# Adding the sent expert rows to the shared expert's rows by accumulating transfers of GpSimd's queue

## The chip, the cores and the metric

The kernel runs on one core of one Trainium2 chip. The metric is the device time of one execution in microseconds (us), the median of several runs. Its engines are TensorE (PE in the profile; PEld is its weight load), VectorE (DVE), ScalarE (ACT), GpSimd (POOL) and SyncE (SP), which does nothing here but issue transfers. GpSimd and ScalarE issue transfers as well. SPq in the rows is SyncE's queue.

## What is computed

One decoder layer for 512 tokens of width 1024, all in float32: a mixer (attention and short convolution), and then a mixture of experts with a shared expert. Only the second half matters here:

```python
h = h + rms_norm(mix, post_mix_norm)
t = rms_norm(h, pre_ffn_norm)                       # 512 tokens x 1024
# each token: the best of 4 groups, and in it the 2 best of 8 experts, weights combine[n, e]
hid = silu(t @ w_gate[e]) * (t @ w_up[e]) * combine[:, e]        # 32 experts, 256 wide
routed = sum over the chosen e of hid @ w_down[e]
shared = (silu(t @ w_sh_gate) * (t @ w_sh_up)) @ w_sh_down
out = h + rms_norm(routed + shared, post_ffn_norm)
```

So each token has two routed rows of 1024 numbers, one from each of its two experts, and one shared row.

## The kernel before

**Experts by pairs.** The 32 experts are worked off in 16 pairs by `pairs_gen`. A pair gathers up to 64 tokens of each of its two experts into 128 partitions (tile `xg`, by an indirect transfer from `t_d` in HBM), multiplies them with the two experts' weights (PSUM tile `pgu`, then `pht`, then `pdn`), and gets 128 finished rows (tile `yb`). For the first 15 pairs `send` puts these rows into `y_d` in HBM with an indirect transfer of GpSimd's queue. `y_d` has 1024 rows: row k\*512 + n holds what token n got from its k-th expert, k = 0 or 1. Rows that have no place there, those of the last pair among them, stay zero.

**Weights.** SyncE's queue loads each expert's three weight tiles of 1024 KB (`ld (e, i)`; i = 2 is the down projection) in the order in which `queue_load` puts them down, into a pool of 25 slots. The last two weights are `ld (31, 2)` and `ld (15, 2)`. Behind them come `gp` (the norm's gain), four loads `kk0` to `kk3` of 1024 KB each, and two loads `hb0` and `hb1` of 1024 KB, which hold the residual h. `kk{c}` brings both `y_d` rows of the 128 tokens of block c side by side. A `kk` load may only be put into the queue once the last send has been issued (`ok=lambda: "sent" in cv`).

**The end.** `shared_gen` has left the shared expert's rows in SBUF, two tiles `sho`, of which `acc(c)` is the part of token block c (c = 0 to 3). The last pair's rows don't go through `y_d`: `last_gen` keeps them in `ys`, split into a high and a low part, and a one-hot matrix `sel` spreads them over the tokens by a product. For each block c and each half of the columns one PSUM bank `pca` adds up three things: the shared rows (`inject`, product of the identity with `acc(c)`), the last pair's rows (product of `sel` with `ys`) and the sent rows (VectorE adds the two halves of `kk{c}`, and a product of the identity with that sum closes the bank). Then ScalarE squares the bank for the norm, VectorE multiplies it with the gain into `tm`, GpSimd raises the mean square to the power -0.5 (`rf`), VectorE adds the residual (`store`, into `hb`), and SyncE writes the block out in two halves.

**Order.** Each engine works off its instructions in the order in which the generators issue them; `run` picks the next generator by estimated times while the program is built. GpSimd's queue is such an order too: a transfer that waits there holds up what stands behind it. At run time an instruction starts when what it waits for has come.

Nearly all instructions are issued through one helper at line 159 (line 314 for products), so tiles, not lines, tell them apart.

Of the kernel before, what the change touches and what calls it, by code (L numbers as in the profile page):

```python
# [13 lines left out]
OP = mybir.AluOpType  # L14
# [4 lines left out]
P = 128  # L19
# [146 lines left out]
def hymba_kernel(ctx: ExitStack, tc: tile.TileContext, xT, xmT, x, meta, cpk, pos, wqkv, wconv, wuq, wukv,  # L166
# [123 lines left out]
    def free_bank(n=1):  # L290
        def f():
            if len(banks) + n <= NBANK:
                return 0.0
            return sorted(done(b) for b in banks)[len(banks) + n - NBANK - 1]
        return f
# [7 lines left out]
    def flag(d, *names):  # L303
        return lambda: 0.0 if all(n in d for n in names) else INF
# [4 lines left out]
    def every(*needs):  # L309
        return lambda: max(f() for f in needs)  # L310
# [64 lines left out]
    def queue_load(name, src, n=2048, ok=None):  # L375

        Slots.queue.append((name, src, n, ok))
# [22 lines left out]
        if j == S_AT:  # L400
            queue_load((NE, 2), we[NE, 2])
    queue_load("gp", g_post[None, :].to_broadcast([P, D]), D)
    for c in range(NT):
        queue_load(f"kk{c}", y_d[:, :].rearrange("(k c p) d -> c p k d", k=2, c=NT)[c], ok=lambda: "sent" in cv)
        if c % 2:
            queue_load(f"hb{c // 2}", h_d[c // 2 * 256:(c // 2 + 1) * 256, :].rearrange("(q p) d -> p q d", p=P))


    jp = m1.bitcast(I32)[:, 0:P]
# [672 lines left out]
    def acc(c):  # L1082
        return sh["out"][c // 2][:, (c % 2) * D:(c % 2 + 1) * D]
# [299 lines left out]
    def overflow():  # L1383

        n = nc.values_load(ov["novf"][0:1, 0:1], min_val=0, max_val=16)  # L1385
        with tc.If(n > 0):
            for half in range(2):
                for c in range(NT):
                    combine(rt["ys"], sel, HALF[half], c)
            for c in range(NT):  # L1390
                V.tensor_tensor(acc(c), acc(c), fin["kk"][c][:, :D], op=OP.add)
            with tc.For_i(0, n, 1) as i:
                overflow_tile(i)
            post_again()
# [62 lines left out]
    def pairs_gen():  # L1457
        wk_, yb, ys, box = rt["wk"], rt["yb"], None, None
        rt["jk"] = wk_.bitcast(BF)[:, 3584:3584 + 512]
        xt_ = wk_[:, :D]  # L1460
        sg, hd, ht = (wk_[:, D + q * 256:D + (q + 1) * 256] for q in range(3))
        yield every(at(xg[0]), free_bank(2))
        xpose(xg[0], xt_)
        gather(2)
        first = NP - PE_PAIRS
        for j, es in enumerate(pairs):
            ps = None
            for i in range(2):
                yield every(loaded(*((e, i) for e in es)), free_bank())
                w = [got((e, i)) for e in es]  # L1470
                yield at(*w, xt_)
                if ps is None:
                    ps = bank("pgu")
                for k in range(4):
                    col2(ps, xt_[:, (4 * i + k) * P:(4 * i + k + 1) * P],
                         [w[q][:, k * 512:(k + 1) * 512] for q in range(2)], i + k == 0, i + k == 4)
                rel(*w)
            hidden(ps, wgt[:, j:j + 1], sg, hd)
            sh["silu"] = True
            if j == S_GO:  # L1480
                sh["go"] = True
            if j == first:
                box = reserve("ys", dt=F32R)
                rel(yb)
                yield lambda: 0.0 if box else INF
                rt["ys"] = ys = box[0]
            if j + 1 < NP:
                yield every(at(xg[(j + 1) % 2]), free_bank(2))
                xpose(xg[(j + 1) % 2], xt_, V)
            if j + 3 < NP:  # L1490
                gather(j + 3)
            if j == NP - 1:
                yield every(flag(sh, "done"), free_bank(2))
                inject(0)
            yield every(at(hd), free_bank())
            hidden_t(hd, ht)
            if j >= first:
                V.tensor_tensor(sel.rearrange("p (c n) -> p c n", c=NT), iop[:, None, :].to_broadcast([P, NT, P]),
                                tok[:, :, j:j + 1].to_broadcast([P, NT, P]), op=OP.is_equal)
            if j == NP - 1:  # L1500
                spawn(last_gen(es), 5)
                return
            yield every(loaded(*((e, 2) for e in es)), free_bank(2))
            w = [got((e, 2)) for e in es]
            yield at(*w, ht)
            for half in range(2):
                ps = down(half, ht, [t[:, half * D:(half + 1) * D] for t in w])
                if j >= first:
                    y_out(ps, ys, HALF[half])
                else:  # L1510
                    o = yb[:, j % 2 * D:(j % 2 + 1) * D][:, HALF[half]]
                    if half:
                        V.tensor_copy(o, ps)
                    else:
                        S.activation(o, ps, AF.Copy)
            rel(*w)
            if j < first:
                send(j, yb[:, j % 2 * D:(j % 2 + 1) * D])
            if j == first - 1:
                cv["sent"] = True  # L1520

    def send(j, y):

# [11 lines left out]
    def inject(c):  # L1535

        for half in range(2):
            pa[c, half] = bank("pca")
            held.append(pa[c, half])
            mm(pa[c, half], ident, acc(c)[:, HALF[half]], start=True, stop=False)  # L1540

    def last_gen(es):


        ys, ht = rt["ys"], rt["wk"][:, D + 512:D + 768]
        ss, rf = small([P, 2 * NT], "ssf"), small([P, NT], "rf")
        var = small([P, 2 * NT], "var")
        kk = {}
        yield every(loaded(*((e, 2) for e in es)), free_bank(2))
        w = [got((e, 2)) for e in es]  # L1550
        yield at(*w, ht)
        for half in range(2):
            y_out(down(half, ht, [t[:, half * D:(half + 1) * D] for t in w]), ys, HALF[half])
        rel(*w)
        yield free_bank(2)
        inject(1)
        tm = reserve("tm0", "tm1")
        yield every(loaded("gp"), lambda: 0.0 if len(tm) == 2 else INF)
        gp, hb = got("gp"), {}
        fin.update(gp=gp, tm=tm, kk=kk)  # L1560

        def rows(c):

            kk[c] = got(f"kk{c}")
            V.tensor_tensor(kk[c][:, :D], kk[c][:, :D], kk[c][:, D:2 * D], op=OP.add)

        def tmc(c, o=slice(0, D)):
            return tm[c // 2][:, c % 2 * D:(c % 2 + 1) * D][:, o]

        def store(c):  # L1570
            if c % 2 == 0:
                hb[c // 2] = got(f"hb{c // 2}")
            h = hb[c // 2][:, c % 2 * D:(c % 2 + 1) * D]
            for q in HALF:
                V.scalar_tensor_tensor(h[:, q], tmc(c, q), rf[:, c:c + 1], h[:, q], op0=OP.mult, op1=OP.add)
                Y.dma_start(out[c * P:(c + 1) * P, q], h[:, q])

        yield loaded("kk0")
        rows(0)
        for c in range(NT):  # L1580
            if c >= 2:
                yield free_bank(2)
                inject(c)
            yield at(ys)
            for half in range(2):
                for q in range(2):
                    mm(pa[c, half], sel[:, c * P:(c + 1) * P], ys[:, q * D + half * 512:q * D + (half + 1) * 512],
                       start=False, stop=False)
            yield at(kk[c])
            for half in range(2):  # L1590
                mm(pa[c, half], ident, kk[c][:, HALF[half]], start=False, stop=True)
            if c + 1 < NT:
                yield loaded(f"kk{c + 1}")
                rows(c + 1)
            for half in range(2):
                S.activation(rt["jk"], pa[c, half], AF.Square, accum_out=ss[:, 2 * c + half:2 * c + half + 1])
                V.tensor_tensor(tmc(c, HALF[half]), pa[c, half], gp[:, HALF[half]], op=OP.mult)
            v = var[:, 2 * c:2 * c + 2]
            V.tensor_scalar(v[:, 0:1], ss[:, 2 * c:2 * c + 1], 1.0 / D, EPS, op0=OP.mult, op1=OP.add)
            V.scalar_tensor_tensor(v[:, 1:2], ss[:, 2 * c + 1:2 * c + 2], 1.0 / D, v[:, 0:1], op0=OP.mult, op1=OP.add)  # L1600
            G.tensor_tensor(rf[:, c:c + 1], v[:, 1:2], neghalf[:, 0:1], op=OP.pow)
            for half in range(2):
                held.remove(pa[c, half])
            if c:
                yield loaded(f"hb{(c - 1) // 2}") if c % 2 else None
                store(c - 1)
        store(NT - 1)
# [94 lines left out]
```

## Time and profile before

| | |
|---|---|
| median of 3 runs | 510.53 us (510.01 to 511.55) |
| the profiled execution | 509.86 us |
| its span | 508.1 us |
| PE busy | 481.9 us, 95% of the span |
| DVE busy | 226.6 us, 45% |
| ACT busy | 164.0 us, 32% |
| POOL busy | 88.0 us, 17% |

The span is what the trace covers, from the first instruction to the last; the execution's own time is 1.8 us longer. All moments below are microseconds from the span's start in this one execution. PE's busy share says little by itself, since products are pipelined and their ends modelled; what bounds the end of the kernel has to be read from the waits there.

### The profile page before, as it was taken

To read this page: it belongs to the slowest core of one execution; us is meant where nothing else is said; L and a number is where in the kernel's file an instruction comes from. 1 tells how busy PE (TensorE), PEld (TensorE's weight loads), DVE (VectorE), ACT (ScalarE), POOL (GpSimd) and SP (SyncE) were. 2 spreads that over 40 slices of the span, in tenths; PEclk is the share of its full clock that TensorE was granted. 3 is DMA by queue.
4 is the path that set the end of the run, shared out by engine and by line. 5 is a ranking of instruction groups with operands and counts; after the bars stand their busy time and mean duration, and the time that the engine had idled before them with its cause. 6 is when DMAs were issued, how large, how long until landed. Compare 5 with 4: busy or idle time off the path is not lost. (4 is left out here: it accounts for less than half of the span.)

```text
span 508.1 us, 7246 instructions
## 1 busy us (share of the span) xinstructions
PE 481.9 (95%) x2766; PEld 304.0 (60%) x2766; DVE 226.6 (45%) x522; ACT 164.0 (32%) x334; POOL 88.0 (17%) x114
## 2 busy tenths in 40 slices
PE   7999999999999999999999999999999988898893
PEld 7998999788767788898944333433333332233251
DVE  6477789656877632578831210101111101011075
ACT  6775526445345642442121211311111110011131
POOL 2034234400000002560211110011111110100011
PEclk9999999999999999999999999999999999999998
DMA  8952240090207588399379999999999999999994
GB/s 296 394 244 83 84 166 0 36 379 1 84 2 292 210 348 331 133 367 414 131 285 389 422 426 415 422 421 418 422 419 418 420 420 418 418 422 422 393 388 158
DMA packets 30309, 151.30 MB, mean 298 GB/s; under 512 B 5480, under 2 KB 5864, under 8 KB 16192
## 3 DMA queue, kind: packets, MB, share of 16 engines
q1 hardware_dynamic: 24512, 138.43, 67.9%
q0 software_dynamic: 4464, 8.17, 4.4%
q10 hardware_dynamic: 1296, 4.21, 2.1%
q8 instruction: 23, 0.38, 0.3%
q14 instruction: 14, 0.11, 0.1%
HBM read 140.54 MB, written 18.35 MB: 313 GB/s over the span
## 5 line engine op out<-in xcount | busy, mean ns | idle before, releaser
L314 PE MATMUL pc<-xh,cw 128*128 128x256 f32 (+2 forms) x320 | 70.0, 309 | 0.0
L159 DVE SCALAR_TENSOR_TENSOR wk<-wk,wgt,pgu 128x256 f32<-128x256 f32 x16 | 7.7, 480 | 118.0 <-ACT wk L159 118.0
L314 PEld LDWEIGHTS pc<-xh,cw 128*128 128x128 f32 x320 | 52.3, 189 | 4.0 <-issue 1.3
L159 ACT ACTIVATE wk<-pgu 128x256 f32<-128x256 f32 x16 | 6.2, 385 | 141.3 <-PE pgu L314 141.3
L314 PE MATMUL pc<-xl,cw 128*128 128x256 f32 (+2 forms) x160 | 48.8, 305 | 0.0
L159 POOL DMA_INDIRECT xg<-t_d,idx x16 | 17.0, 1064 | 114.4 <-PE pxt L314 69.8
L159 DVE COPY yb<-pdn 128x512 f32<-128x512 f32 x15 | 10.4, 692 | 59.3 <-PE pdn L314 59.3
L159 POOL DMA_INDIRECT y_d<-yb,sidx x15 | 15.1, 1008 | 95.6 <-DVE yb L159 68.9
L314 PEld LDWEIGHTS pc<-xl,cw 128*128 128x128 f32 x160 | 30.3, 189 | 1.2
L159 ACT ACTIVATE att<-pS,nm 128x128 f32<-128x128 f32 (+3 forms) x32 | 16.9, 528 | 29.3 <-DVE nm L159 27.1
L314 PE MATMUL pS<-kT,qT 128*128 128x128 f32 (+3 forms) x64 | 22.7, 440 | 0.0
L159 POOL TENSOR_TENSOR sst<-rst,neghalf 128x1 f32<-128x1 f32 x12 | 7.6, 635 | 81.5 <-DVE rst L159 78.1
L314 PEld LDWEIGHTS pxt<-ident,xg 128*128 128x128 f32 x128 | 14.0, 141 | 11.3 <-issue 7.8
L314 PE MATMUL pco<-wo,cvh 128*128 128x512 f32 x64 | 20.6, 403 | 0.0
L314 PE MATMUL pao<-wo,mgh 128*128 128x512 f32 x64 | 20.0, 393 | 0.0
L159 POOL TENSOR_TENSOR cw<-ld conv,cw 128x1024 fp32r<-128x1024 f32 x6 | 15.6, 2612 | 18.5 <-ACT cw L159 18.5
L314 PE MATMUL psh<-tT,ld (32, 0)_1930 128*128 128x128 f32 x128 | 18.8, 280 | 0.0
L159 ACT ACTIVATE yb<-pdn 128x512 f32<-128x512 f32 x15 | 9.0, 597 | 28.0 <-PE pdn L314 28.0
L314 PE MATMUL psh<-tT,ld (32, 1)_1932 128*128 128x128 f32 x128 | 17.8, 277 | 0.0
L314 PE MATMUL pxt<-ident,xg 128*128 128x128 f32 x128 | 17.3, 278 | 0.0
L314 PEld LDWEIGHTS psh<-tT,ld (32, 0)_1930 128*128 128x128 f32 x128 | 16.2, 192 | 0.2 <-issue 0.2
L159 DVE TENSOR_REDUCE nm<-pS 128x1 f32<-128x128 f32 (+3 forms) x32 | 15.5, 483 | 1.7 <-PE pS L314 1.4
(486 smaller groups left out, 1192.0 us busy)
## 6 DMA issues: line engine op xcount, KB each, us to landing
ld conv<-in_wconv_dram SPq DMA_DIRECT2D x6, 1024.0 KB, 9.9
ld out<-in_wout_dram SPq DMA_DIRECT2D x4, 1024.0 KB, 5.0
y_d<-sel SPq DMA_DIRECT2D x4, 1024.0 KB, 7.2
ld kk<-y_d SPq DMA_DIRECT2D x4, 1024.0 KB, 10.0
xs<-in_x_dram SPq DMA_DIRECT2D x4, 512.0 KB, 9.2
x<-in_x_dram SPq DMA_DIRECT2D x4, 512.0 KB, 5.2
h_d<-mix ACTq DMA_DIRECT2D x4, 512.0 KB, 5.4
t_d<-x ACTq DMA_DIRECT2D x4, 512.0 KB, 6.6
```

Of the source, the lines that this page charges most:

```text
L159: r = f(*a, **k)
L314: f(o, *ins, **kw)
```

## The change

The sent rows are no longer loaded and no longer go through VectorE and a product. Instead eight transfers of GpSimd's queue read 128 rows of `y_d` each (512 KB) and add them, on their way, to `acc(c)` in SBUF (`accum_op=OP.add`), two for each block c. A one-element copy on GpSimd (tile `gate`) reads the tile `ld (31, 2)` ahead of them, so none of them is issued before that weight has landed. `inject` now closes the bank in place of opening it, and stands behind the transfers' end; the products with `sel` open it. `hb0` and `hb1` are queued right behind `gp`, with no condition.

```diff
     queue_load("gp", g_post[None, :].to_broadcast([P, D]), D)
-    for c in range(NT):
-        queue_load(f"kk{c}", y_d[:, :].rearrange("(k c p) d -> c p k d", k=2, c=NT)[c], ok=lambda: "sent" in cv)
-        if c % 2:
-            queue_load(f"hb{c // 2}", h_d[c // 2 * 256:(c // 2 + 1) * 256, :].rearrange("(q p) d -> p q d", p=P))
+    for c in range(2):
+        queue_load(f"hb{c}", h_d[c * 256:(c + 1) * 256, :].rearrange("(q p) d -> p q d", p=P))
...
-            if j == NP - 1:
-                yield every(flag(sh, "done"), free_bank(2))
-                inject(0)
...
     def inject(c):
 
         for half in range(2):
-            pa[c, half] = bank("pca")
-            held.append(pa[c, half])
-            mm(pa[c, half], ident, acc(c)[:, HALF[half]], start=True, stop=False)
+            mm(pa[c, half], ident, acc(c)[:, HALF[half]], start=False, stop=True)
...
         w = [got((e, 2)) for e in es]
+
+        G.tensor_copy(small([P, 1], "gate"), w[0][:, 0:1])
+        for c, k in ((0, 0), (1, 0), (0, 1), (2, 0), (1, 1), (3, 0), (2, 1), (3, 1)):
+            G.dma_start(acc(c), y_d[k * SEQ + c * P:k * SEQ + (c + 1) * P, :], accum_op=OP.add)
         yield at(*w, ht)
...
-        yield free_bank(2)
-        inject(1)
...
-        yield loaded("kk0")
-        rows(0)
-        for c in range(NT):
-            if c >= 2:
-                yield free_bank(2)
-                inject(c)
-            yield at(ys)
+        def onehot(c):
             for half in range(2):
+                pa[c, half] = bank("pca")
+                held.append(pa[c, half])
                 for q in range(2):
                     mm(pa[c, half], sel[:, c * P:(c + 1) * P], ys[:, q * D + half * 512:q * D + (half + 1) * 512],
-                       start=False, stop=False)
-            yield at(kk[c])
-            for half in range(2):
-                mm(pa[c, half], ident, kk[c][:, HALF[half]], start=False, stop=True)
-            if c + 1 < NT:
-                yield loaded(f"kk{c + 1}")
-                rows(c + 1)
+                       start=q == 0, stop=False)
+
+        yield every(at(ys), free_bank(4))
+        onehot(0)
+        onehot(1)
+        for c in range(NT):
+            if c + 1 < NT and c:
+                yield free_bank(2)
+                onehot(c + 1)
+            yield at(acc(c))
+            inject(c)
             for half in range(2):
                 S.activation(rt["jk"], pa[c, half], AF.Square, accum_out=ss[:, 2 * c + half:2 * c + half + 1])
-                V.tensor_tensor(tmc(c, HALF[half]), pa[c, half], gp[:, HALF[half]], op=OP.mult)
+            V.tensor_tensor(tmc(c, HALF[0]), pa[c, 0], gp[:, HALF[0]], op=OP.mult)
...
             G.tensor_tensor(rf[:, c:c + 1], v[:, 1:2], neghalf[:, 0:1], op=OP.pow)
+            V.tensor_tensor(tmc(c, HALF[1]), pa[c, 1], gp[:, HALF[1]], op=OP.mult)
```

The first place is GpSimd's queue at the end of the program: `y_d<-yb` are the last sends, `sho` are the tiles of the shared rows (blocks 0 and 1 in `sho_2849`, 2 and 3 in `sho_2850`), and `rf` is the power of the norm. Lines with + are new, the others stand in both.

```order
 L159 DMA y_d<-yb,sidx 1024x1024 x3
+L159 COPY gate<-ld (31, 2)_3496 128x1
+L159 DMA sho_2849<-y_d 128x1024 x3
+L159 DMA sho_2850<-y_d 128x1024
+L159 DMA sho_2849<-y_d 128x1024
+L159 DMA sho_2850<-y_d 128x1024 x3
 L159 TENSOR_TENSOR rf<-var,neghalf 128x1 x4
```

Eight transfers now stand between the last send and the four `rf`. The transfers of one block add to the same bytes, so the second of a block waits until its first has landed, and it holds up everything behind it in this queue.

The second place is PE's order from the last pair's down projection (`pdn`) to the end. First the kernel before; one `inject` (`pca<-sho`) stands ahead of `pht` and so ahead of these rows:

```order
L314 MATMUL pdn<-ld (15, 2)_3498,wk 64x512
L314 MATMUL pca<-sho_2849,ident 128x512 x2
L314 MATMUL pca<-ys,sel 128x512 x4
L314 MATMUL pca<-ld kk_3638,ident 128x512 x2
L314 MATMUL pca<-ys,sel 128x512 x4
L314 MATMUL pca<-ld kk_3640,ident 128x512 x2
L314 MATMUL pca<-sho_2850,ident 128x512 x2
L314 MATMUL pca<-ys,sel 128x512 x4
L314 MATMUL pca<-ld kk_3644,ident 128x512 x2
L314 MATMUL pca<-sho_2850,ident 128x512 x2
L314 MATMUL pca<-ys,sel 128x512 x4
L314 MATMUL pca<-ld kk_3646,ident 128x512 x2
```

And PE after the change, from the same row:

```order
L314 MATMUL pdn<-ld (15, 2)_3498,wk 64x512
L314 MATMUL pca<-ys,sel 128x512 x8
L314 MATMUL pca<-sho_2849,ident 128x512 x2
L314 MATMUL pca<-ys,sel 128x512 x4
L314 MATMUL pca<-sho_2849,ident 128x512 x2
L314 MATMUL pca<-ys,sel 128x512 x4
L314 MATMUL pca<-sho_2850,ident 128x512 x4
```

The four groups of products on `kk` are gone, and all four groups on `sho` now stand behind `ys` and behind the transfers into `sho`.

## Rows read from the trace of the kernel before

**Rows 1.** The page's head.

```profile
span 508.1 us, 7246 instructions
```

**Rows 2.** The chain that ended last: start, duration, engine, tile.

```profile
499.74 0.59 ACT wk L159
...
501.32 1.43 DVE ld hb L159 x2
...
503.31 0.75 DVE ld hb L159 x2
```

**Rows 3.** PE's timeline, 483 to 500: start, duration, operation, count of records.

```profile
483.62 1.99 PE L314 MATMUL pca<-sho,ident 128*128 128x512 f32 x4
485.04 1.48 PE L314 MATMUL pca<-ys,sel 128*128 128x512 f32 x4
...
490.74 1.88 PE L314 MATMUL pca<-sho,ident 128*128 128x512 f32 x4
...
493.39 1.88 PE L314 MATMUL pca<-ld kk,ident 128*128 128x512 f32 x4
495.11 1.88 PE L314 MATMUL pca<-sho,ident 128*128 128x512 f32 x4
...
497.76 1.88 PE L314 MATMUL pca<-ld kk,ident 128*128 128x512 f32 x4
```

**Rows 4.** DVE's timeline, 484 to 492; in brackets idle time and its end.

```profile
484.37 0.69 DVE L159 TENSOR_TENSOR ys<-pdn,ys 128x512 fp32r<-128x512 f32 x1 [1.03 <-ACT ys L159]
...
490.81 1.23 DVE L159 TENSOR_TENSOR ld kk<-ld kk 128x1024 f32<-128x1024 f32 x1 [0.81 <-DMA ld kk<-y_d]
```

**Rows 5.** Timeline of SyncE's queue, 455 to 478: when transfers were issued.

```profile
455.89 0.33 SPq L159 DMA_DIRECT2D ld (31, 2)_3496<-in_we_dram  x1
458.38 0.33 SPq L159 DMA_DIRECT2D ld (15, 2)_3498<-in_we_dram  x1
461.37 0.33 SPq L159 DMA_DIRECT2D ld gp<-in_g_post_dram  x1
477.24 0.90 SPq L159 DMA_DIRECT2D ld kk<-y_d  x2
```

**Rows 6.** Waits of SyncE's queue from 420: total, times, longest.

```profile
SPq L159 <- DMA y_d<-yb,sidx: 15.5, 1, 15.5
```

**Rows 7.** Transfers issued from 440 on: size, us from issue to landing.

```profile
ld (31, 2)_3496<-in_we_dram SPq DMA_DIRECT2D x1, 1024.0 KB, 20.9
ld (15, 2)_3498<-in_we_dram SPq DMA_DIRECT2D x1, 1024.0 KB, 20.9
ld gp<-in_g_post_dram SPq DMA_DIRECT2D x1, 512.0 KB, 19.2
```

**Rows 8.** GpSimd's timeline from 460.

```profile
469.11 0.98 POOL L159 DMA_INDIRECT y_d<-yb,sidx  x1 [14.43 <-DVE yb L159]
...
493.57 1.04 POOL L159 TENSOR_TENSOR rf<-var,neghalf 128x1 f32<-128x1 f32 x1 [2.91 <-DVE var L159]
```

**Rows 9.** The last send, issued in 469 to 471: us to landing.

```profile
y_d<-yb,sidx POOLq DMA_INDIRECT x1, 8.1
```

**Rows 10.** Gathers issued in 247 to 260, with the transfers' rate there.

```profile
DMA packets 464, 1.34 MB, mean 103 GB/s; under 512 B 190, under 2 KB 190, under 8 KB 412
...
xg<-t_d,idx POOLq DMA_INDIRECT x2, 4.0
```

**Rows 11.** The page's transfer queues: packets, MB, share; q0 is GpSimd's.

```profile
q0 software_dynamic: 4464, 8.17, 4.4%
```

**Rows 12.** Windows: from:to, length, busy time (instructions) by engine, PEclk, transfer share, GB/s.

```profile
466.00:470.00 4.00, 3.71 (x16) 1.05 (x14) 0.69 (x1) 0.55 (x1) 0.89 (x1) 1.00 1.02 424
477.00:495.00 18.00, 17.47 (x55) 8.12 (x55) 10.49 (x18) 5.21 (x13) 1.61 (x2) 1.00 0.96 381
```

**Rows 13.** Windows behind PE's last product, columns as in rows 12.

```profile
499.00:502.50 3.50, 0.64 (x2) 0.00 (x0) 2.70 (x6) 1.25 (x4) 1.00 (x1) 1.00 0.39 146
...
503.50:504.00 0.50, 0.00 (x0) 0.00 (x0) 0.50 (x1) 0.00 (x0) 0.00 (x0) 0.50 0.98 377
```

More of the change, by code (lines that the diff above doesn't have):

```diff
@@ L1389, in overflow @@
                     combine(rt["ys"], sel, HALF[half], c)
-            for c in range(NT):
-                V.tensor_tensor(acc(c), acc(c), fin["kk"][c][:, :D], op=OP.add)
             with tc.For_i(0, n, 1) as i:
@@ L1518, in pairs_gen @@
                 send(j, yb[:, j % 2 * D:(j % 2 + 1) * D])
-            if j == first - 1:
-                cv["sent"] = True
     def send(j, y):
@@ L1547, in last_gen @@
         var = small([P, 2 * NT], "var")
-        kk = {}
         yield every(loaded(*((e, 2) for e in es)), free_bank(2))
         w = [got((e, 2)) for e in es]
+        G.tensor_copy(small([P, 1], "gate"), w[0][:, 0:1])
+        for c, k in ((0, 0), (1, 0), (0, 1), (2, 0), (1, 1), (3, 0), (2, 1), (3, 1)):
+            G.dma_start(acc(c), y_d[k * SEQ + c * P:k * SEQ + (c + 1) * P, :], accum_op=OP.add)
         yield at(*w, ht)
@@ L1559, in last_gen @@
         gp, hb = got("gp"), {}
[L1560 to L1565, printed above, removed]
+        fin.update(gp=gp, tm=tm)
         def tmc(c, o=slice(0, D)):
@@ L1576, in store @@
                 Y.dma_start(out[c * P:(c + 1) * P, q], h[:, q])
-        yield loaded("kk0")
-        rows(0)
-        for c in range(NT):
-            if c >= 2:
-                yield free_bank(2)
-                inject(c)
-            yield at(ys)
+        def onehot(c):
             for half in range(2):
+                pa[c, half] = bank("pca")
+                held.append(pa[c, half])
                 for q in range(2):
                     mm(pa[c, half], sel[:, c * P:(c + 1) * P], ys[:, q * D + half * 512:q * D + (half + 1) * 512],
-                       start=False, stop=False)
-            yield at(kk[c])
-            for half in range(2):
-                mm(pa[c, half], ident, kk[c][:, HALF[half]], start=False, stop=True)
-            if c + 1 < NT:
-                yield loaded(f"kk{c + 1}")
-                rows(c + 1)
+                       start=q == 0, stop=False)
[8 more added lines that the diff above has]
+            inject(c)
             for half in range(2):
                 S.activation(rt["jk"], pa[c, half], AF.Square, accum_out=ss[:, 2 * c + half:2 * c + half + 1])
-                V.tensor_tensor(tmc(c, HALF[half]), pa[c, half], gp[:, HALF[half]], op=OP.mult)
+            V.tensor_tensor(tmc(c, HALF[0]), pa[c, 0], gp[:, HALF[0]], op=OP.mult)
             v = var[:, 2 * c:2 * c + 2]
```

## The prediction

> **What bounds the kernel now.** First the page's head: the span is 508.1 us [rows 1], and the profiled execution took 509.86 us, so 1.8 us lie outside it. The change touches only the last 30 us, so I read that stage and no average. The chain that ended last [rows 2] starts at 499.74 with ScalarE's square of the last PSUM half and runs over VectorE's residual adds to 504.06; then the last block is stored. Whatever moves the end of PE's last product, at 497.76 + 1.88 = 499.64, moves the end of the kernel by as much.
>
> What sets that moment? PE's timeline [rows 3]: from 485.04 the groups of products follow each other without a gap. From one `inject` to the next, 490.74 to 495.11, is 4.37 us for one block: its three groups, of which the one on `kk` takes 1.72 us (start 493.39 to the next start 495.11). They start at the moment at which `ys` is ready, 484.37 + 0.69 = 485.06 [rows 4]. So the last 15 us are PE's, and the loads of `kk` keep up with it only just: VectorE waited 0.81 us for one of them [rows 4].
>
> Behind that stands the transfers' own limit. SyncE's queue stood still for 15.5 us [rows 6] until the last send, issued at 469.11 and landing 8.1 us later at 477.2 [rows 8, 9], and issued the first `kk` at 477.24 [rows 5]. In 477 to 495 the transfers moved 381 GB/s, and 424 where the weights stream undisturbed [rows 12]. So two things end near each other: PE's products and 4 MB of sent rows.
>
> **The change, part by part.**
>
> *Removed.* Four groups on `kk`, 4 x 1.72 = 6.9 us of PE, and four adds on VectorE of 1.23 us each [rows 4], which lie beside PE's work. But two of the four `inject` groups, which ran before `ys` was ready (one of them at 483.62 [rows 3]), now stand behind it: +2 x 1.72. If the sums in `acc` were always there in time, PE would end 3.4 us earlier, at 496.2. That is the most that PE can give.
>
> *The gate.* `ld (31, 2)` lands at 455.89 + 20.9 = 476.8 [rows 5, 7]; a one-element GpSimd instruction takes about 1.0 us at most [rows 8]. The first addition has to wait for the last send's landing, 477.2, anyway. I start it at 477.3.
>
> *What is on the way beside it.* `ld (15, 2)` lands at 479.3, `gp` at 480.6 [rows 5, 7]; the two `hb` now come right behind, 1.05 MB each, 2.5 us each at 424 GB/s, so about 485.6 if nothing disturbs them. At 477.3 that is 8.3 us of work in front of or beside the additions. The four `kk` loads and the eight additions read the same 4.19 MB.
>
> *The eight additions.* Each costs GpSimd 1.0 us to issue, as a send does [rows 8]. The trace has no adding transfer. The nearest rows are the sends and gathers of the same queue: 8.1 us from issue to landing with the weights streaming beside it [rows 9], 4.0 us in a stretch that moved only 103 GB/s [rows 10]. Those carry 8.17 MB in 31 transfers (16 gathers, 15 sends), 0.26 MB each [rows 11]; an addition has 0.52 MB, 0.6 us more at 424 GB/s, so 4.6 us in the free. Call the latency of an addition L, between 4.6 and 8.1 us. Then the queue's order gives: (block 0, first) issued 477.3, landed 485.4; (1, first) 478.3, landed 486.4, both beside the loads. (0, second) has to wait until 485.4, (2, first) goes at 486.4, (1, second) at 487.4, (3, first) at 488.4. (3, second) waits until (3, first) has landed, 488.4 + L, and lands at 488.4 + 2L. With L = 4.6 that is 497.6, with 8.1 it is 504.6.
>
> The other bound is bytes. After 477.3 there are 3.47 MB of loads and 4.19 MB of additions: 18.1 us at 424 GB/s, no landing of the last before 495.4. If adding occupies the transfer engines twice as long as copying, since it has to read its target too, it is 8.2 + 19.8 us, 505.3. I take L = 6.3, the middle: two or three additions are always in flight and share the engines, which a lone gather does not show, but the loads end before the second half. The last addition then lands at 501.0.
>
> *After it.* The last `inject`, 1.88 us [rows 3], ends at 502.9 in place of 499.64: **+3.3 us**. What follows is the same chain as in [rows 2]; swapping one gain product with the norm's small steps doesn't shorten it, since VectorE works without a break there.
>
> *What is queued behind.* The four `rf` now stand behind all eight issues in GpSimd's queue, so the first can run only when (3, second) has been issued: 494.7 + 1.0, and it takes 1.0 [rows 8]. VectorE's residual adds wait for it, two blocks' worth of them, 2 x 1.43 [rows 2], with one block's gain products between them, two of about 0.7 as VectorE's other pass over such a bank [rows 4]: done at about 501. The last block's products need VectorE only at about 502. So this costs nothing, with 1 us to spare; without it, it costs at most that chain's overhang.
>
> *At nothing:* `pht` no longer stands behind an `inject`, so the last down projection may start half a us earlier, if `ld (15, 2)` is there; that only lengthens PE's wait. The early `hb` is needed after the first `rf`.
>
> *A rule against the row.* A lone gather in the free took 4.0 us for 0.26 MB [rows 10]. The Trainium skill ("DMA: Bandwidth & Descriptors", "Anatomy of one DMA — SWDGE (gpsimd) path") fits such a transfer by 2.0 us + bytes / 436 GB/s, an estimate of 3.2 us for an addition. By that the eighth would land at about 490, ahead of PE, and the time would be that of the rival "faster". The trace disagrees: 4.0 us for half the bytes, and 8.1 beside the loads.
>
> The sum: 509.86 + 3.3 = 513.2. The runs' median is 0.7 above the profiled execution, so I predict **513.8 us**.
>
> **The rivals.**
>
> *Same:* the additions cost what copies do and find free engines from 486 on, L = 4.6. The last lands at 497.6, PE ends at 499.5, the time is 510.4. For it: the loads that could disturb end at 485.6. Against it: the first two additions push them back by 2.5 us.
>
> *Faster:* the queue keeps the transfer engines full and the bytes alone decide. The last lands at 495.4, PE ends at 497.3, -2.3: 508.2. From a landing at 497.7 on the change loses. For it: the dip while SyncE waited (381 against 424 GB/s) is filled by `hb`. Against it: in the second half each of two chains has one addition to wait for before the next is issued.
>
> *Dear additions:* the read of the target doubles the engines' time. The last lands at 505.3, PE ends at 507.2, +7.6: 518.1. Nothing in the trace of before excludes it. The Trainium skill ("DMA: Bandwidth & Descriptors", "Rules for kernel authors") says that the accumulate reads its destination and writes it later; no run here shows it so far.
>
> *A slow clock on top:* the granted clock stood at 1.00 (2.4 GHz) until 502.5 and at 0.50 (1.2 GHz) from 503.5, after PE's last product at 499.64 [rows 13]. PE will now wait from about 487.0 (485.1 and two groups on `ys`, 4.37 - 2 x 1.72 = 0.93 each) for the first sum, which comes at 491.7 (485.4 + 6.3), long enough for that. If the clock is still low at the last `inject`, this takes 3.8 us: +1.9, and with dear additions 520.0.
>
> **How the numbers follow.** Forecast (L from 5.4 to 8.1, landing 499.3 to 504.6, 511.9 to 517.5): 0.47. Dear additions or a slow clock: 0.15. Same: 0.20. Faster: 0.18. 0.3% of 510.5 is 1.5 us, about what these runs can tell apart; +1.5 us is a landing at 499.3, -1.5 one at 496.2. So slower 0.62, same 0.20, faster 0.18. The range reaches from the faster rival, 508.0, to dear additions with a slow clock, 520.0; beyond both I leave 0.15. If it is slower, 512 to 520.
>
> **What would show it.** The eight additions on GpSimd's queue with gaps that end on an addition's landing; landings of 5 to 8 us; PE idle in front of `pca<-sho`, ended by a transfer and not by `ys`; the last of these starting near 501; `rf` late but not in the chain. I am wrong if PE has no gap there (then the bytes or PE decide), if the weights' last landing moves past 479.3 (then the gate is too early), or if additions land in under 4.6 or over 10 us.

## The result, and the profile after

The changed kernel takes 519.17 us (median of 4 runs, 518.66 to 520.02), beside it the kernel before 510.5 us (4 runs, 510.01 to 511.55): a ratio of 1.0165, 95% interval 1.0151 to 1.0178. It is 8.7 us slower. I had forecast 513.8 us, slower, with a range up to 520.0: the sign is right, the size is not. The profiled execution took 519.4 us.

From the page of the changed kernel, the span, and of the transfer queues the row of GpSimd's queue (packets, MB, share of 16 engines' span), which answer to [rows 1, 11]:

```profile
span 517.7 us, 7212 instructions
...
q0 software_dynamic: 5616, 12.36, 8.6%
```

This second row already shows the price. The queue carries 12.36 - 8.17 = 4.19 MB more, the eight additions. Its time goes from 4.4% of 508.1 us, 22.4 us of all 16 engines, to 8.6% of 517.7 us, 44.5 us. So 4.19 MB took 22.1 us of all engines: 190 GB/s, less than half of the 424 GB/s at which the weights stream [rows 12].

The chain that ended last, from 477 on (start, duration, what), which answers to [rows 2]:

```profile
477.50 0.76 POOL sho L159
478.26 11.68 DMA sho<-y_d
489.94 0.29 issue
490.23 0.55 POOL sho L159
490.77 10.50 DMA sho<-y_d
501.27 0.28 issue
501.56 5.71 DMA sho<-y_d
507.26 0.04 issue
507.31 1.14 PE pca L314 x2
...
512.11 1.41 DVE ld hb L159 x2
```

Three additions stand in it one behind another: issued, landed, and on its landing the next is issued. They take 11.7, 10.5 and 5.7 us. The last has the engines nearly to itself; the others share them. In the prediction's terms these are (1, first), (3, first) and (3, second), and L was to be 6.3.

GpSimd's timeline from 476 (idle time and what ended it in brackets), which answers to [rows 8]:

```profile
476.93 0.18 POOL L159 COPY gate<-ld (31, 2)_3496 128x1 f32<-128x1 f32 x1 [6.82 <-DMA ld (15, 2)_3498<-in_we_dram]
477.50 1.92 POOL L159 DMA_DIRECT2D sho<-y_d  x2 [0.39 <-DMA y_d<-yb,sidx]
486.80 1.77 POOL L159 DMA_DIRECT2D sho<-y_d  x2 [7.38 <-DMA sho<-y_d]
490.23 1.77 POOL L159 DMA_DIRECT2D sho<-y_d  x2 [1.66 <-DMA sho<-y_d]
496.09 0.88 POOL L159 DMA_DIRECT2D sho<-y_d  x1 [4.09 <-DMA sho<-y_d]
501.56 0.87 POOL L159 DMA_DIRECT2D sho<-y_d  x1 [4.59 <-DMA sho<-y_d]
```

The gate opens in time and takes 0.18 us. Then come the gaps that the prediction named, each ended by an addition's landing, but the steps are late: the third addition is issued at 486.8 (forecast 485.4), the last at 501.56 (forecast 494.7).

PE's timeline from 484, which answers to [rows 3]:

```profile
484.77 1.43 PE L314 MATMUL pca<-ys,sel 128*128 128x512 f32 x5 [0.23 <-DVE ys L159]
493.12 3.79 PE L314 MATMUL pca<-sho,ident 128*128 128x512 f32 x4 [6.92 <-DMA sho<-y_d]
495.92 2.67 PE L314 MATMUL pca<-ys,sel 128*128 128x512 f32 x4
498.94 1.99 PE L314 MATMUL pca<-sho,ident 128*128 128x512 f32 x4 [0.35 <-DMA sho<-y_d]
500.36 1.50 PE L314 MATMUL pca<-ys,sel 128*128 128x512 f32 x4
503.76 1.98 PE L314 MATMUL pca<-sho,ident 128*128 128x512 f32 x4 [1.91 <-DMA sho<-y_d]
507.31 1.98 PE L314 MATMUL pca<-sho,ident 128*128 128x512 f32 x4 [1.56 <-DMA sho<-y_d]
```

Where the groups of products stood back to back before, PE now waits for an addition ahead of every `inject`, 10.7 us in all. It ends at 507.31 + 1.98 = 509.29 in place of 499.64: +9.65 us, and the span grew by 9.6. What follows PE's last product is unchanged: 8.4 us to the span's end, 8.5 before.

Windows of the changed kernel (columns as in [rows 12]: busy time by engine, PEclk, transfer share, GB/s):

```profile
466.00:470.00 4.00, 3.54 (x16) 1.02 (x14) 0.69 (x1) 0.58 (x1) 0.85 (x1) 1.00 1.02 422
482.00:484.00 2.00, 2.00 (x10) 0.48 (x6) 0.69 (x1) 0.87 (x2) 0.00 (x0) 1.00 1.02 260
488.00:490.00 2.00, 0.00 (x0) 0.00 (x0) 0.00 (x0) 0.00 (x0) 0.57 (x1) 0.55 1.00 215
494.00:496.00 2.00, 2.00 (x5) 0.83 (x3) 0.04 (x1) 0.69 (x2) 0.00 (x0) 0.50 1.05 201
502.00:504.00 2.00, 0.24 (x1) 0.24 (x2) 1.43 (x3) 0.00 (x0) 1.57 (x3) 1.00 0.68 78
504.00:506.00 2.00, 1.75 (x4) 0.44 (x3) 0.79 (x2) 0.84 (x3) 0.00 (x0) 1.00 1.04 205
```

The engines are full (share about 1.00) almost all the way, but what they move falls from 422 to 260 GB/s as the additions come beside the loads, and to some 205 once only additions are left. Only around 502, where the eighth addition is issued late, do they idle for a moment. So the transfers bound the end, by their engines' time; the experiments test this reading.

### The profile page after: what moved, and what is told of

Read it like the earlier page. It is cut to its first block, busy times and chain, and to the rows that moved or that the text cites. A ratio compares the mean times of both kernels' runs of the same rounds, so it can differ in the third digit from the quotient of the medians.

```text
span 517.7 us, 7212 instructions
## 1 busy us (share of the span) xinstructions
PE 480.1 (93%) x2750; PEld 301.9 (58%) x2750; DVE 221.5 (43%) x518; ACT 163.9 (32%) x334; POOL 93.3 (18%) x123
## 3 DMA queue, kind: packets, MB, share of 16 engines
q0 software_dynamic: 5616, 12.36, 8.6%
## 4 chain that ended last, share of the span: by engine, by line
PE 61%; DMA 34%; DVE 3%; issue 1%; ACT 0%; POOL 0%; SPq 0%; ACTq 0%
PE pc L314 13%; PE pgu L314 7%; DMA sho<-y_d 5%; PE psh L314 5%; PE pco L314 4%; DMA ld (7, 2)_3007<-in_we_dram 4%; PE pao L314 4%; DMA ld (11, 2)_3238<-in_we_dram 4%; DMA ld (26, 1)_3161<-in_we_dram 4%; DMA ld (13, 0)_3340<-in_we_dram 4%; DMA ld (9, 0)_3080<-in_we_dram 4%; PE pq L314 4%; DMA ld (30, 1)_3421<-in_we_dram 4%; PE pS L314 4%; DMA ld (15, 2)_3498<-in_we_dram 4%; PE pdn L314 3%
## 5 line engine op out<-in xcount | busy, mean ns | idle before, releaser
L314 PE MATMUL pca<-sho,ident 128*128 128x512 f32 x16 | 9.7, 739 | 10.7 <-DMA sho<-y_d 10.7
L314 PE MATMUL pxt<-ident,xg 128*128 128x128 f32 x128 | 17.3, 278 | 0.0
L314 PEld LDWEIGHTS psh<-tT,ld (32, 0)_1930 128*128 128x128 f32 x128 | 16.2, 192 | 0.2 <-issue 0.2
```

The source lines that it names most:

```text
L314: f(o, *ins, **kw)
```

## The experiments

Four explanations for the 8.7 us were set against each other. **A**: an addition occupies the transfer engines about twice as long as a copy, and that sets the end. **B**: the waits of GpSimd's queue set it (an addition to the same block has to wait for the first one, and holds up the rest). **C**: TensorE's low clock at the first `inject` sets it. **D**: the `hb` loads, now ahead of the additions, set it. Each edit is to the changed kernel unless said otherwise; each ratio is to the kernel before, run beside it.

**1. Copies in place of additions** (`e1_copy`). The same transfers in the same order with the same waits; the sums are left out.

```diff
-            G.dma_start(acc(c), y_d[k * SEQ + c * P:k * SEQ + (c + 1) * P, :], accum_op=OP.add)
+            G.dma_start(acc(c), y_d[k * SEQ + c * P:k * SEQ + (c + 1) * P, :])
```

> The changed kernel with the adding left out: the same eight transfers in the same order and with the same waits, but they copy the rows of y_d over acc(c), so the sums are not the reference's. Theory A (adding occupies the transfer engines twice as long as copying): the windows that show about 205 GB/s with a transfer share of 1.0 go back to about 400 GB/s, the last transfer lands near 497 in place of 507.3, and the time falls by 8 to 10 us, to 509 to 511 us. Theory B (the waits of one transfer for another in GpSimd's queue make the length): they are all still there, so the time stays at 516 us or more.

Measured: 511.94 us (10 runs, 511.29 to 512.98), the kernel before 510.41; ratio 1.0025 (1.0012 to 1.0037). 7.2 of the 8.7 us are gone; the time is 0.9 us above A's range. The page's row of GpSimd's queue in this kernel (span 511.2 us):

```profile
q0 software_dynamic: 5616, 12.36, 6.7%
```

That is 34.3 us of 16 engines, so 11.9 us for the same 4.19 MB, against 22.1 as additions: 1.9 times. And a window of it:

```profile
492.00:494.00 2.00, 2.00 (x5) 0.88 (x4) 0.75 (x2) 0.85 (x3) 0.01 (x1) 0.50 1.03 377
```

Copies from the same queue move 377 GB/s at full share where additions move 205. The waits in GpSimd's queue are all still there, each shorter:

```profile
485.77 1.06 POOL L159 DMA_DIRECT2D sho<-y_d  x2 [6.56 <-DMA sho<-y_d]
487.76 1.07 POOL L159 DMA_DIRECT2D sho<-y_d  x2 [0.93 <-DMA sho<-y_d]
491.47 0.54 POOL L159 DMA_DIRECT2D sho<-y_d  x1 [2.64 <-DMA sho<-y_d]
495.04 0.54 POOL L159 DMA_DIRECT2D sho<-y_d  x1 [3.02 <-DMA sho<-y_d]
```

A holds, B as the sole cause falls. Copies also cost GpSimd less to issue, 0.54 us against 0.88; three issues stand in the chain of the changed kernel, so this can be about 1 of the 7.2 us. What is left, 1.5 us above the kernel before, says that in this form the plan would not have won even with additions at a copy's price.

**2. Half of them additions** (`e5_half`). The first transfer of each block adds, the second copies; sums are left out, waits are the same.

```diff
-            G.dma_start(acc(c), y_d[k * SEQ + c * P:k * SEQ + (c + 1) * P, :], accum_op=OP.add)
+            G.dma_start(acc(c), y_d[k * SEQ + c * P:k * SEQ + (c + 1) * P, :],
+                        **({} if k else {"accum_op": OP.add}))
```

> The changed kernel with the first transfer of each block adding and the second one copying over it (its sums are left out), in the same order and with the same waits. Theory A (engine time of an addition is twice that of a copy): half of the difference between the eight additions (519.2) and the eight copies (511.9) is gone, 515.5 us, within 514.5 to 516.7. Theory B (waits in the queue): all waits are kept, 518 us or more.

Measured: 516.69 us (4 runs, 514.67 to 516.84), the kernel before 510.83; ratio 1.0102 (1.0078 to 1.0125), between the two and at the upper edge of A's range. The page's row of the queue (span 515.1 us):

```profile
q0 software_dynamic: 5616, 12.36, 7.7%
```

39.7 us, so 17.3 us for the 4.19 MB: between 11.9 and 22.1, the middle being 17.0. The engines' time goes with the number of additions, as A says; it is not a price of the queue or of its waits. All additions here have one size, so whether it goes by bytes or by packets is not shown.

**3. The order with shorter waits** (`e2_order`). All first additions ahead of all second ones, so that a second one finds its first one landed or nearly so.

```diff
-        for c, k in ((0, 0), (1, 0), (0, 1), (2, 0), (1, 1), (3, 0), (2, 1), (3, 1)):
+        for c, k in ((0, 0), (1, 0), (2, 0), (3, 0), (0, 1), (1, 1), (2, 1), (3, 1)):
```

> The changed kernel with the eight additions in another order: all four first ones, then all four second ones, so that a second one finds its first one landed or nearly so. Theory A: the bytes and their double cost stay, the last landing stays within 505 to 507.5, the time within 517 to 519.5 us. Theory B: the two chains of waits get shorter, the time falls by 3 us or more, to 516 us or less.

Measured: 521.21 us (4 runs, 519.94 to 521.42); ratio 1.021 (1.0188 to 1.0232). No gain: it is 2.0 us slower than the changed kernel and 1.7 us above A's range. GpSimd still waits four times for a landing, 12.1 us in all against 17.7. Windows (columns as above) and PE's timeline of this kernel:

```profile
492.00:494.00 2.00, 0.00 (x0) 0.00 (x0) 0.00 (x0) 0.00 (x0) 0.71 (x1) 0.50 1.06 209
502.00:504.00 2.00, 2.00 (x7) 1.00 (x6) 0.76 (x2) 0.90 (x4) 0.57 (x1) 1.00 0.66 131
504.00:506.00 2.00, 2.00 (x8) 1.23 (x7) 1.86 (x5) 0.73 (x3) 0.55 (x1) 1.00 0.09 18
```

```profile
498.02 3.40 PE L314 MATMUL pca<-sho,ident 128*128 128x512 f32 x4 [11.96 <-DMA sho<-y_d]
...
504.84 3.59 PE L314 MATMUL pca<-sho,ident 128*128 128x512 f32 x8
```

The additions do end about 2 us earlier (share 0.66 in 502 to 504 and 0.09 behind it, where the changed kernel still has 1.04 until 506), so B has a part in when the last one lands. But the engines move the same 209 GB/s, and all four first additions go ahead of the second ones, so the four blocks get their sums late together: the first `inject` starts at 498.02, not 493.12. Most of the blocks' closing work then stands behind the transfers and not beside them. The longer waits in the queue are the price for finishing blocks one by one, and shortening them bought nothing here.

**4. The residual's loads behind the additions** (`e3_late_h`). `hb0` and `hb1` are issued behind the fourth and the sixth addition (a fill of one column by GpSimd holds them back).

```diff
-    for c in range(2):
-        queue_load(f"hb{c}", h_d[c * 256:(c + 1) * 256, :].rearrange("(q p) d -> p q d", p=P))
...
+            if k == 0 and c >= 2:
+                t = Slots.have[f"hb{c - 2}"] = slot(f"ld hb{c - 2}")
+                G.memset(t[:, 0:1], 0.0)
+                Y.dma_start(t[:, :2048].rearrange("p (q d) -> p q d", q=2),
+                            h_d[(c - 2) * 256:(c - 1) * 256, :].rearrange("(q p) d -> p q d", p=P))
```

> The changed kernel with the two loads of h issued only behind the fourth and the sixth addition, in place of being queued from 464 on (a one-element write by GpSimd into their tiles makes them wait). Theory A: the engines have the same work in another order, the last addition lands within 505 to 508, the time stays within 517.5 to 520 us. Theory D (the early loads of h in front of and beside the first additions are what delays the row of additions): the first two additions land at 484 and 487 in place of 486.8 and 490, and the time falls by 3 us or more.

Measured: 520.7 us (4 runs, 520.2 to 522.5); ratio 1.0196 (1.0173 to 1.0218). This is 0.7 us above A's range. GpSimd's queue went on behind the first two additions at 483.4 and 486.4, as D had said, and yet the time did not fall: D falls as a cause here. The first two `inject` start earlier (488.79 and 497.87 in place of 493.12 and 498.94), the third later (505.70 in place of 503.76): what no longer stands ahead of the additions stands beside the last of them. A window with additions alone, and PE's last group:

```profile
482.00:484.00 2.00, 1.95 (x9) 0.56 (x5) 0.83 (x2) 0.71 (x2) 0.59 (x2) 1.00 1.05 197
```

```profile
505.70 6.44 PE L314 MATMUL pca<-sho,ident 128*128 128x512 f32 x8 [3.37 <-DMA sho<-y_d]
```

With no load beside them the additions still move only 197 GB/s: the low rate is theirs, not that of two queues that disturb each other. The last two `inject` then run together at the low clock (6.44 us for eight records, granted clock 0.50 in 506 to 508), and PE ends at 512.14 in this execution (the slowest of the four, 522.5 us), 2.9 us after the changed kernel's.

**5. Filler products while PE waits** (`e4_warm`). Six products into a bank that nobody reads, behind the first two groups on `ys`.

```diff
+        pw = bank("pwarm")
+        for _ in range(6):
+            mm(pw, ident, gp[:, :512], start=True, stop=True)
```

> The changed kernel with six products of the identity with gp into a spare PSUM bank (nobody reads it) between the second group on ys and the first inject, so that PE has about 5 us of work where it waits. Theory A: the granted clock stays at 1.00 from 487 to 493 and the first inject takes 1.9 in place of 3.8 us, but the last addition lands when it did, so the time is the same within 0.5 us. Theory C (the low clock is part of the loss): the time falls by 1.5 us or more.

Measured: 519.52 us (4 runs, 519.17 to 520.76); ratio 1.0184 (1.0158 to 1.021), the changed kernel's time. PE's first and last `inject`:

```profile
493.42 1.99 PE L314 MATMUL pca<-sho,ident 128*128 128x512 f32 x4 [1.77 <-DMA sho<-y_d]
...
507.07 1.98 PE L314 MATMUL pca<-sho,ident 128*128 128x512 f32 x4 [1.73 <-DMA sho<-y_d]
```

The clock stays at 1.00 past the first `inject`, which takes 1.99 us and not 3.79 (it falls later, at the second one, with time to spare). The last one starts as late as in the changed kernel, 507.07 against 507.31, since it waits for its transfer. C falls.

**6. Copies with filler products** (`e6_copy_warm`). Experiment 1 with three such products. Sums are left out.

```diff
-            G.dma_start(acc(c), y_d[k * SEQ + c * P:k * SEQ + (c + 1) * P, :], accum_op=OP.add)
+            G.dma_start(acc(c), y_d[k * SEQ + c * P:k * SEQ + (c + 1) * P, :])
...
+        pw = bank("pwarm")
+        for _ in range(3):
+            mm(pw, ident, gp[:, :512], start=True, stop=True)
```

> The kernel with eight copies in place of the additions (sums left out) and three products of the identity with gp into a spare PSUM bank behind the second group on ys. With copies PE stood without a gap from 489.95 to 501.5, at the low granted clock until 495, so there the clock should be in the chain: Theory C for this kernel says that the granted clock stays at 1.00, the first inject takes 1.9 in place of 3.8 us, and the time falls by 1 to 2 us, to 510 to 511 us. If the clock does not matter there either, it stays at 511.9.

Measured: 511.15 us (10 runs, 509.35 to 511.82), the kernel before 510.83; ratio 1.0004 (0.9993 to 1.0015), against 1.0025 in experiment 1. The time lies between the two forecasts, nearer to C's 510 to 511. With copies PE stands in the chain that ended last, for 7.22 us in experiment 1 and 4.68 us here, and its clock seems to cost about 1 us of the time; the two intervals overlap a little, so this size is not settled. The kernel before is only matched.

**7. The early `hb` in the kernel before** (`e7_h_early`, an edit of the kernel before). The two `hb` loads go ahead of the four `kk`.

```diff
+    for c in range(2):
+        queue_load(f"hb{c}", h_d[c * 256:(c + 1) * 256, :].rearrange("(q p) d -> p q d", p=P))
     for c in range(NT):
         queue_load(f"kk{c}", y_d[:, :].rearrange("(k c p) d -> c p k d", k=2, c=NT)[c], ok=lambda: "sent" in cv)
-        if c % 2:
-            queue_load(f"hb{c // 2}", h_d[c // 2 * 256:(c // 2 + 1) * 256, :].rearrange("(q p) d -> p q d", p=P))
```

> The kernel before with one part of the change alone: the two loads of h are queued right behind gp, ahead of the four loads of the sent rows. Theory D (queued early, the 2.1 MB of h are paid by what comes behind them): the first kk lands about 3 us later, PE waits for it behind the products on ys, the time rises by 2 to 3.5 us to 512.5 to 514 us. Its rival (the early loads only fill the dip in which SyncE waited for the last send): the time stays within 0.5 us of before.

Measured: 515.15 us (4 runs, 514.86 to 515.85); ratio 1.0088 (1.0068 to 1.0108), 4.3 us slower by the medians and above the 2 to 3.5 us that D had forecast. VectorE's wait for the first `kk`, and PE behind it:

```profile
488.47 1.23 DVE L159 TENSOR_TENSOR ld kk<-ld kk 128x1024 f32<-128x1024 f32 x1 [3.06 <-DMA ld kk<-y_d]
```

```profile
489.75 2.80 PE L314 MATMUL pca<-ld kk,ident 128*128 128x512 f32 x4 [2.86 <-DVE ld kk L159]
491.56 2.69 PE L314 MATMUL pca<-ys,sel 128*128 128x512 f32 x4
```

In that execution PE ends at 504.73 in place of 499.64, +5.1. PE's wait is 2.86 us of it. Most of the rest lies in two slower groups, the `kk` group (2.80 us against 1.88 [rows 3]) and the `ys` group behind it (2.69 against 1.48 [rows 3]), both in part at a granted clock of 0.50; groups overlap, so these differences only add up roughly. So the early `hb` is dear in the kernel before, where PE then works without a gap to the end. In the changed kernel, where the transfers' total decides, delaying `hb` gained nothing (experiment 4).

**8. The sums on GpSimd** (`b1_pool_sum`, an edit of the kernel before, as a way to win). The four `kk` loads stay, with `hb` behind them. For blocks 2 and 3 GpSimd adds the first expert's rows to `acc`, VectorE the second's, and one product with the identity serves both; PE's order follows.

```diff
+            if c < 2:
+                kk[c] = got(f"kk{c}")
+                V.tensor_tensor(kk[c][:, :D], kk[c][:, :D], kk[c][:, D:2 * D], op=OP.add)
+            else:
+                V.tensor_tensor(acc(c), acc(c), kk[c][:, D:2 * D], op=OP.add)
+
+        def first(c):
+
             kk[c] = got(f"kk{c}")
-            V.tensor_tensor(kk[c][:, :D], kk[c][:, :D], kk[c][:, D:2 * D], op=OP.add)
+            G.tensor_tensor(acc(c), acc(c), kk[c][:, :D], op=OP.add)
```

> The kernel before with another way to take work off PE: for blocks 2 and 3 GpSimd adds the first of the two sent rows to the shared rows (128 x 1024, about 2.6 us each by its rows on the convolution weights), VectorE adds the second, and one product with the identity takes the place of two; the loads of h stand behind the four loads of sent rows. By theory A (plain loads cost half of additions, PE's 4.37 us a block are the bound) PE ends 1 to 2 us earlier, VectorE's work is then the next bound: 508.5 to 509.8 us. If GpSimd's additions and VectorE's slow each other or come late: 510.5 us or more.

Measured: 511.17 us (12 runs, 509.74 to 512.35); ratio 1.0005 (0.9993 to 1.0016). No gain. VectorE's timeline, GpSimd's second addition and PE's last group:

```profile
494.35 1.50 DVE L159 SCALAR_TENSOR_TENSOR var<-ssf,var 128x1 f32<-128x1 f32 x1
495.78 1.40 DVE L159 SCALAR_TENSOR_TENSOR ld hb<-tm,rf,ld hb 128x512 f32<-128x512 f32 x2
497.10 1.21 DVE L159 TENSOR_TENSOR sho<-sho,ld kk 128x1024 f32<-128x1024 f32 x1
```

```profile
493.48 2.35 POOL L159 TENSOR_TENSOR sho<-sho,ld kk 128x1024 f32<-128x1024 f32 x1
```

```profile
498.37 2.91 PE L314 MATMUL pca<-sho,ident 128*128 128x512 f32 x4 [2.51 <-DVE sho L159]
```

PE has two groups of products less and now waits 2.51 us for VectorE, which works almost without a gap from 490.5 on. Part of that is the change's own doing: the one-column step at 494.35 took 1.50 us, where the same step took 0.16 at 499.61, and it ended at 495.85, just when GpSimd's addition did (493.48 + 2.35 = 495.83). So VectorE seems to have been held up beside GpSimd's additions, which was the second forecast. By this reading the bound only changed engines; no further run tested it. No version was found that beats the kernel before.

## Why the prediction was right or wrong

**Right.** PE's gain could not be had, since the sums came late. The form of the chain: additions that wait in GpSimd's queue for a landing, PE idle ahead of each `inject`, the end of the kernel one `inject` (1.98 us) and an unchanged tail behind the last landing. The gate cost nothing, and the last weights were not held up: PE's second row of products on `ys` starts at 484.77, where before the first started at 485.04. VectorE waited 0.6 us for a late `rf`, off the chain. The clock did fall to 0.50, but at the first `inject`; at the last it was 1.00, and experiment 5 showed that it costs nothing here.

**A misread row without effect.** The prediction priced an `inject` at 1.72 us of PE and a group on `ys` at 0.93. By the starts of the kernel before, it is otherwise:

```profile
492.06 1.50 PE L314 MATMUL pca<-ys,sel 128*128 128x512 f32 x4
```

With 490.74 before it and 493.39 behind it [rows 3], an `inject` takes 1.32 us and a group on `ys` 1.33. PE's gain would have been about 6.9 - 2 x 1.32 = 4.2 us and not 3.4. As the sums came late, neither entered the forecast's sum.

**Wrong: the step "I take L = 6.3, the middle".** It sized an addition as if it occupied the engines like a copy. The eight took 22.1 us of all 16 engines, 2.8 us each; 4.19 MB at the prediction's 424 GB/s are 9.9 us, 1.2 us each. L was bounded by sends and gathers, 4.6 to 8.1 us, and the prediction reasoned that "the loads end before the second half", after which engines would be free. The loads did end, but additions filled the engines alone. The chain's terms, forecast and measured: the issue of (3, first) 488.4, measured 490.77; then 2L = 12.6, measured 10.50 + 5.71 = 16.2, and 0.3 between the two; the landing 501.0, measured 507.27. The 6.3 us too early are 2.4 + 3.6 + 0.3. The time missed by less, 5.4 us: the prediction added 0.7 us from the profiled execution to the median, but the changed kernel's median lies 0.2 us below its profiled one. Two of the chain's three landings, 11.7 and 10.5 us, also lie over the 10 us from which the prediction called itself wrong.

**The rival that happened** is the dear additions: last landing forecast 505.3, PE's end 507.2, time 518.1; measured 507.27, 509.29 and 519.17 us. Its sum had 8.2 + 19.8 us of engine time; of the 2.0 us on top 0.6 are idle engines around 502 (share 0.68 over 2 us), 0.6 the 205 GB/s in place of the 212 that it had assumed (4.19 MB in 19.8 us), and 0.2 the later start; the other 0.6 I cannot place. It should have had more than a part of 0.15. Nothing in the trace of before spoke against it: no row there shows an addition, so a bound from copies of the same queue bounded only the part of the price that copies have.

By the Trainium skill ("DMA: Bandwidth & Descriptors", "Rules for kernel authors") the accumulate reads its destination and writes it later. The measured 1.9 times a copy's engine time agrees with that; no run here shows the reading itself. The Trainium skill's fit for a transfer of this queue ("DMA: Bandwidth & Descriptors", "Anatomy of one DMA — SWDGE (gpsimd) path") gives 3.2 us for the bytes of an addition, as an estimate. It does not hold here: the shortest in the chain took 5.7 us.

**Where the 10 us of engine time went.** As copies the transfers need 22.1 - 11.9 = 10.2 us less of all engines, but only 7.2 us of time came back in experiment 1. In 477.3 to 498.3 of that kernel the share is 0.88, so the engines idle for 2.5 us of it and no longer bound the end. Its chain that ended last shows what does:

```profile
485.77 4.14 DMA sho<-y_d
489.91 0.04 issue
489.95 7.22 PE pca L314 x12
```

It leaves the transfers at 489.91, with block 0's second copy, and goes on over PE, which is at the low clock at first (0.50 in 492 to 494), and over VectorE to the end. With copies the bound has moved to the work behind the first sum, so more engine time saved could not come back. B is real but second in line: its waits are worth about 2 us at the additions' end (experiment 3), which that order lost again behind it.

Open is why an addition takes the engines 1.9 times as long (a second pass over the target, or something else in each packet); and no run had additions on another queue or with other packet sizes.

## What to carry to other kernels

An operation "on the way" is not free when the way is the bound: price a changed transfer by its engines' time per byte first (here some 205 GB/s for additions against 377 for copies of the same queue), and by its latency second. Where the transfer engines are full anyway, a shorter wait in a queue need not bring time, and it may end the overlap with the work behind (experiment 3). And if no row of the profile shows the operation, measure a copy in its place: that one run told the two apart.

## What was not expected of the hardware

- Additions alone moved some 190 to 215 GB/s with the transfer engines fully busy, in three kernels with different numbers of them in flight (experiments 3 and 4 and the changed kernel); copies by the same queue moved 377.
- Issuing an addition took GpSimd 0.88 us, a copy of the same shape 0.54 us.
- GpSimd's copy of a 128x1 tile took 0.18 us, its power on the same shape 0.55 (the changed kernel) to 1.04 [rows 8].
- A one-column step of VectorE took 1.50 us while GpSimd added 128x1024 beside it, and 0.16 us otherwise (experiment 8).
